# A two-layer decoder trunk: all products with the activations stationary, norms by rows, contracted operands turned on TensorE

## The chip, the cores and the metric

The kernel runs on one core of a Trainium2 chip, with its five engines: TensorE (matrix products and transposes), VectorE, ScalarE, GpSimd and SyncE, which issues most DMA transfers. The metric is device time in microseconds (us), the median of several runs.

## The reference

256 tokens of width 2048 pass two layers, in float32. Layer 0 is a gated spatial mixer, layer 1 attention with 16 heads of 128. With 256 tokens and key blocks of 256 every query's own block is the only one, so that layer is plain causal attention.

```
layer 0: u, v = gelu(x @ w_in[:, :4096]); z = x @ w_in[:, 4096:]
         v = layer_norm(v); s = tril(w_s[g]) @ v + b_s[g]     # 16 groups, 128-token chunks
         y = u * s * silu(z)
layer 1: q, k, v, z = x @ w_in;  y = causal_attention(q, k, v) * silu(z)
both:    x = layer_norm(alpha * x + y @ w_out[i])
         x = x + sigmoid(x @ w_gate[i]) * (p[i] @ w_proj[i])
```

## The kernel before

Weights stream through the core once, in 180 chunks of 128 x 2048 numbers (1 MiB). A chunk is loaded in two pieces by SyncE's queue into one of four buffers `wr` (L102), and every number is split exactly into hi (12 significant bits, `wh`, by ScalarE, L103) and lo (the rest, `wl`, by VectorE, L104). Loads and splits are issued two chunks ahead of the products (`AHEAD`); `wh` and `wl` have three buffers each. For the first two chunks of each gate matrix (`POOL_LO`) GpSimd makes the lo. A float32 product runs as three passes in a faster format, hi x hi, hi x lo and lo x hi, which add up in a bank of PSUM (eight banks of 128 x 512).

Activations lie feature-major, features on partitions and tokens along the row, except `v` in both layers. There are two kinds of products:

- `column_units` (L144 to L166, all its products have line L162): a chunk of 128 output columns and all 2048 input rows. The weights are stationary, the activations move. For each of the 16 contraction tiles one product with `wh` moves hi and lo of the activations together (512 columns), one with `wl` moves the hi alone (256): 32 products a chunk. The two halves of the bank are added on the way out by ScalarE and VectorE (`halves_sum`, L169, L170). u and z of layer 0, q, k and z of layer 1, w_out and the gate (`w_gate`) of both layers are made so, 144 chunks.
- `row_unit` (L172 to L198, products L184, L186, L188): the activations are stationary and the weights move, 512 columns at a time: 24 products a chunk. The output has tokens on partitions. Only `v` of layers 0 and 1 (banks `v`, `y`) is made so, 32 chunks.

The order of the program is that of the code, refined by a scheduler when the kernel is built. `tick` runs after every chunk of products, and `at(n, f)` puts `f` behind the n-th chunk from there: so the spatial mixing (`spatial`, L293, L294, after `mixing_bias`, L240, L241), the softmax steps of a head (`scores` L532 to L551, `probs` L557, `values` L572) run between products of other chunks. Each engine takes its instructions strictly in order.

The LayerNorm of a layer (`after`, from L336) is feature-major, so its sums run over partitions. VectorE and ScalarE gather sums of the residual and its square while w_out runs; a product with a matrix of 1/2048 (`st`, L412 to L414) gives the moments; `diag` (L424, L429), GpSimd's power (L427) and a product with ones (`rb`, L452) bring 1/sigma to all partitions. Meanwhile TensorE runs `embed`, p @ w_proj (L444 to L446, bank `pp`): five of its eight steps ahead of `rb`, three behind. Then `norm_pair` (L460 to L467) makes the input `xn` of the gate.

Of the kernel before, what the change touches and what calls it, by code (L numbers as in the profile page):

```python
# [30 lines left out]
NT4 = 21           # 4 KB tiles of activations on chip: (hi, lo) of what products take  # L31
NT2 = 18           # 2 KB tiles
# [7 lines left out]
def decoder_trunk(ctx: ExitStack, tc: tile.TileContext, xT, pT, wv_a, wu_a, wz_a, w_sT, b_s,  # L40
                  wv_b, wqkz_b, w_out, w_gate, w_proj, cols, out):
    """Activations lie feature-major ([features, tokens]) all the way, except v, by rows in both
    mixers. Every float32 product runs as three float32r passes: an operand is split exactly into
    hi (12 significant bits) + lo (the rest), and hi*hi + hi*lo + lo*hi add up in PSUM."""
# [4 lines left out]
    small = ctx.enter_context(tc.tile_pool(name="small", bufs=4))  # L49
    psum = ctx.enter_context(tc.tile_pool(name="psum", bufs=8, space=bass.MemoryType.PSUM))  # L50
# [6 lines left out]

    def bank(name):
# [20 lines left out]
    on_pool = set()  # L79
# [64 lines left out]
    def column_units(n, xs, step=KT, joined=False):  # L144
# [502 lines left out]
```

## Time and profile before

| | us |
|---|---|
| Median of three runs | 1076.09 (1075.79 to 1077.84) |
| Profiled execution, first to last instruction (span) | 1075.3 |
| TensorE busy | 1057.4 (98% of the span) |
| VectorE busy | 719.0 (67%) |
| ScalarE busy | 528.5 (49%) |
| GpSimd busy | 29.2 (3%) |
| DMA | 198.71 MB, mean 185 GB/s |

The profiled execution is one run of the program; its own time is known as the span, which lies 0.8 us under the median of the runs. Busy times are shares of the whole, over stages with different limits. A product's duration includes its way through the array, in which the next one already runs: prices of products are read from start to start, or from the chain.

### The profile page before, as it was taken

To read this page: it belongs to the slowest core of one execution; us is meant where nothing else is said; L and a number is where in the kernel's file an instruction comes from. 1 tells how busy PE (TensorE), PEld (TensorE's weight loads), DVE (VectorE), ACT (ScalarE), POOL (GpSimd) and SP (SyncE) were. 2 spreads that over 40 slices of the span, in tenths; PEclk is the share of its full clock that TensorE was granted. 3 is DMA by queue.
4 is the path that set the end of the run, shared out by engine and by line. 5 is a ranking of instruction groups with operands and counts; after the bars stand their busy time and mean duration, and the time that the engine had idled before them with its cause. 6 is when DMAs were issued, how large, how long until landed. Compare 5 with 4: busy or idle time off the path is not lost.

```text
span 1075.3 us, 15279 instructions
## 1 busy us (share of the span) xinstructions
PE 1057.4 (98%) x5946; PEld 918.8 (85%) x5946; DVE 719.0 (67%) x1103; ACT 528.5 (49%) x787; POOL 29.2 (3%) x28
## 2 busy tenths in 40 slices
PE   8999999999999989999999999999999999998998
PEld 6888888888888878888888888888888888897887
DVE  5567866756577988665545666666666566889664
ACT  5455534445534466554434654555555543456542
POOL 1100000000000040000000000000000000022000
PEclk9999999999999989999999999999999999998999
DMA  7984545455755526555555545444455555452761
GB/s 259 292 272 159 194 163 187 163 193 181 260 196 189 186 96 206 186 196 195 195 195 178 176 159 173 159 172 161 160 179 177 190 194 190 176 187 83 254 211 49
DMA packets 59000, 198.71 MB, mean 185 GB/s; under 512 B 6560, under 2 KB 8864, under 8 KB 58928
## 3 DMA queue, kind: packets, MB, share of 16 engines
q1 hardware_dynamic: 58896, 197.68, 53.2%
q8 instruction: 47, 0.77, 0.3%
q14 instruction: 25, 0.20, 0.1%
q0 software_dynamic: 32, 0.05, 0.0%
HBM read 195.61 MB, written 2.10 MB: 184 GB/s over the span
## 4 chain that ended last, share of the span: by engine, by line
PE 95%; DMA 2%; POOL 1%; DVE 1%; issue 1%; SPq 0%; ACT 0%; POOLq 0%; DVEq 0%
PE f L162 76%; PE y L188 3%; PE y L186 3%; PE y L184 3%; PE v L188 2%; PE v L186 2%; PE v L184 2%; POOL wl L104 1%; DVE diag L429 1%; PE ov L572 1%; DMA wr<-in_wv_a 1%; PE pt L557 0%; PE sp L293 0%; DMA xr<-in_xT 0%; DMA wsr<-in_w_sT 0%
## 5 line engine op out<-in xcount | busy, mean ns | idle before, releaser
L104 DVE TENSOR_TENSOR wl<-wr,wh 128x1024 fp32r<-128x1024 f32 (+1 forms) x358 | 424.7, 1203 | 153.5 <-ACT wh L103 152.0
L103 ACT ACTIVATE wh<-wr 128x1024 fp32r<-128x1024 f32 (+1 forms) x366 | 372.8, 1039 | 246.6 <-issue 119.8
L162 PE MATMUL f<-x,wh 128*128 128x512 f32 x1280 | 453.2, 398 | 0.0
L162 PE MATMUL f<-x,wl 128*128 128x256 f32 x1280 | 345.8, 280 | 0.0
L162 PEld LDWEIGHTS f<-x,wh 128*128 128x128 f32 x1280 | 238.2, 188 | 51.3
L162 PEld LDWEIGHTS f<-x,wl 128*128 128x128 f32 x1280 | 241.6, 189 | 5.6
L162 PE MATMUL f<-b,wh 128*128 128x512 f32 (+1 forms) x544 | 179.1, 385 | 0.0
L162 PE MATMUL f<-xn,wh 128*128 128x512 f32 (+1 forms) x544 | 178.8, 385 | 0.0
L162 PE MATMUL f<-b,wl 128*128 128x256 f32 x512 | 139.0, 281 | 0.0
L162 PE MATMUL f<-xn,wl 128*128 128x256 f32 x512 | 139.0, 281 | 0.0
L162 PEld LDWEIGHTS f<-b,wh 128*128 128x128 f32 x544 | 98.4, 188 | 19.6
L162 PEld LDWEIGHTS f<-xn,wh 128*128 128x128 f32 x544 | 98.2, 188 | 19.4
L169 ACT ACTIVATE fp<-f 128x256 f32<-128x256 f32 x78 | 29.3, 379 | 155.4 <-PE f L162 155.4
L162 PEld LDWEIGHTS f<-b,wl 128*128 128x128 f32 x512 | 96.7, 189 | 2.9
L162 PEld LDWEIGHTS f<-xn,wl 128*128 128x128 f32 x512 | 96.8, 189 | 2.8
L170 DVE TENSOR_TENSOR fp<-fp,f 128x256 f32<-128x256 f32 x78 | 32.4, 417 | 85.7 <-ACT fp L169 85.7
L104 POOL TENSOR_TENSOR wl<-wr,wh 128x1024 fp32r<-128x1024 f32 x8 | 19.7, 2478 | 845.8 <-ACT wh L103 845.8
L184 PE MATMUL y<-wh,x 128*128 128x512 f32 x128 | 40.7, 389 | 0.0
L188 PE MATMUL y<-wl,x 128*128 128x512 f32 x128 | 40.7, 389 | 0.0
L186 PE MATMUL y<-wh,x 128*128 128x512 f32 x128 | 40.7, 389 | 0.0
L184 PE MATMUL v<-wh,x 128*128 128x512 f32 x128 | 38.1, 393 | 2.6 <-ACT wh L103 2.6
L188 PE MATMUL v<-wl,x 128*128 128x512 f32 x128 | 37.3, 390 | 0.0
(149 smaller groups left out, 892.2 us busy)
## 6 DMA issues: line engine op xcount, KB each, us to landing
wr<-in_wqkz_b SPq DMA_DIRECT2D x96, 512.0 KB, 3.7
wr<-in_w_out SPq DMA_DIRECT2D x64, 512.0 KB, 3.8
wr<-in_w_gate SPq DMA_DIRECT2D x64, 512.0 KB, 4.2
wr<-in_wu_a SPq DMA_DIRECT2D x32, 512.0 KB, 3.8
wr<-in_wz_a SPq DMA_DIRECT2D x32, 512.0 KB, 3.8
wr<-in_wv_b SPq DMA_DIRECT2D x32, 512.0 KB, 3.8
wr<-in_wv_a SPq DMA_DIRECT2D x26, 512.0 KB, 5.6
wr<-in_w_proj SPq DMA_DIRECT2D x8, 512.0 KB, 3.8
```

Of the source, the lines that this page charges most:

```text
L103: nc.scalar.activation(hi[:, c], raw, AF.Copy)
L104: (nc.gpsimd if len(ready) in on_pool else nc.vector).tensor_sub(lo[:, c], raw, f32(hi[:, c]))
L162: nc.tensor.matmul(*m, start=k == 0 and j == 0, stop=k == KT - 1 and j == len(ms) - 1, skip_group_check=True)
L169: nc.scalar.activation(o, ps[:, 0:S], AF.Copy)
L170: nc.vector.tensor_add(o, o, ps[:, S:2 * S])
L184: nc.tensor.matmul(banks[m][n], xh, wh[:, i, n, :], start=first, stop=False)
L186: nc.tensor.matmul(banks[m][n], xl, wh[:, i, n, :], start=False, stop=False)
L188: nc.tensor.matmul(banks[m][n], xh, wl[:, i, n, :], start=False, stop=last)
L429: nc.vector.tensor_scalar(diag[:, m * P:(m + 1) * P], ident, rv[:, m:m + 1], None, op0=ALU.mult)
L572: nc.tensor.matmul(ov[:, n], vk[m][h // 4][:, a, hc], b, start=j == 0, stop=j == 4, skip_group_check=True)
```

## The change

All products become row-major, with the activations stationary and 512 columns of weights moving; `column_units` is gone. The weights lie in DRAM as before; for a matrix that is stored by columns, a chunk now holds 512 output columns (four blocks `b` of 128) of four contraction tiles `k` (`by_blocks`), so a load's rows are 2 KB where they were 4 KB, and a product's moving operand is four runs of 128 numbers that lie 512 numbers apart. `row_slice` takes four such chunks for 512 columns of all tokens. The results have tokens on partitions, so both norms take statistics along the row (`bn_stats`) and apply gain and bias from broadcast rows `gb`, which `gain_bias` loads by GpSimd's queue from a copy in DRAM (`vecs`). What is contracted next has to be feature-major again: `turn` transposes it on TensorE, four 128x128 tiles a bank, and splits it on the way out. x is turned into rows (`rows_of_x`), q and k of every head into columns (`head`), the output back into columns (`store`). The values product of attention is turned round too. `probs` follows `scores` by one chunk where it was two. GpSimd makes no weight's lo any more.

```diff
+    def by_blocks(w):
+        return [("p (b k c) -> p k b c", dict(b=4, k=4),
+                 w[4 * n:4 * n + 4, :, 512 * c:512 * c + 512].rearrange("b p e -> p b e"))
+                for n in range(NS) for c in range(4)]
+    def flat(src):
+        return [("", {}, src.rearrange("p (b e) -> p b e", b=4))]
...
-            nc.sync.dma_start(raw, src[:, c])
+            nc.sync.dma_start(raw.rearrange("p (b e) -> p b e", b=4 // parts), src[:, b])
             nc.scalar.activation(hi[:, c], raw, AF.Copy)
-            (nc.gpsimd if len(ready) in on_pool else nc.vector).tensor_sub(lo[:, c], raw, f32(hi[:, c]))
-        ready.append((hi, lo))
...
-    def column_units(n, xs, step=KT, joined=False):
...
-                for k in range(k0, k0 + step):
-                    lh = (ps[u][:, 0:S], wl[:, k, :], xs[k][:, 0, :])
...
-                    else:
-                        ms = [(ps[u], wh[:, k, :], xs[k].rearrange("p h s -> p (h s)"))]
-                        ms.insert(k < KT - 1, lh)
-                    for j, m in enumerate(ms):
-                        nc.tensor.matmul(*m, start=k == 0 and j == 0,
-                                         stop=k == KT - 1 and j == len(ms) - 1, skip_group_check=True)
...
-    def halves_sum(o, ps):
-        nc.scalar.activation(o, ps[:, 0:S], AF.Copy)
-        nc.vector.tensor_add(o, o, ps[:, S:2 * S])
...
+        nc.gpsimd.dma_start(vecs, t[0:6 * KT, 0:P])
+    def gain_bias(i, n):
+        t = r4("gb")
+        for j in range(2):
+            v = vecs[(2 * i + j) * KT + 4 * n:(2 * i + j) * KT + 4 * n + 4, :].rearrange("k c -> (k c)")
+            nc.gpsimd.dma_start(t[:, j, :], v.partition_broadcast(P))
+        return t
...
+        pat, kw, wh, wl = weights()
+        if pat:
+            wh, wl = ([w.rearrange(pat, **kw)[:, i] for i in range(len(ks))] for w in (wh, wl))
...
+            def o(n):
+                return banks[m][n].rearrange("p (b c) -> p b c", b=4) if pat else banks[m][n]
...
-                nc.tensor.matmul(banks[m][n], xh, wh[:, i, n, :], start=first, stop=False)
+                nc.tensor.matmul(o(n), xh, wh[i][n], start=first, stop=False)
...
+    def row_slice(xs, name="y"):
+        banks = [[bank(name)] for _ in range(NM)]
+        for c in range(4):
+            row_unit(banks, range(4 * c, 4 * c + 4), xs, both if c == 3 else None)
+        return [b[0] for b in banks]
...
+    def turn(xs, j, rows, n="t"):
+        tp = bank("tp")
+        for u in range(2):
+            f = 2 * j + u
+            for m in range(NM):
+                nc.tensor.transpose(tp[:, u * S + m * P:u * S + (m + 1) * P],
+                                    rows[f // 4][:, m, (f % 4) * P:(f % 4 + 1) * P], ident)
+        t = split(tp, n)
+        xs[2 * j:2 * j + 2] = [t[:, u] for u in range(2)]
...
+    def normalise(r, gb, m, mean, rstd):
+        o = r[:, m, :]
+        nc.vector.scalar_tensor_tensor(o, o, mean, gb[:, 0, :], op0=ALU.subtract, op1=ALU.mult)
+        nc.vector.scalar_tensor_tensor(o, o, rstd, gb[:, 1, :], op0=ALU.mult, op1=ALU.add)
...
-            for m in range(NM):
-                vh, vl = (vs[m][g // 4][:, j, (g % 4) * P:(g % 4 + 1) * P] for j in range(2))
-                nc.tensor.matmul(sp[:, m], vh, w, start=True, stop=False, skip_group_check=True)
-                nc.tensor.matmul(sp[:, m, 0, :], vl, w[:, 0, :], start=False, stop=True,
...
+            vh, vl = (vs[j][:, h, :, i * P:(i + 1) * P] for h in range(2))
+            for a, (wt, vt) in enumerate(((w[:, 0, :], vh), (w[:, 0, :], vl), (w[:, 1, :], vh))):
+                nc.tensor.matmul(sp[:, i], wt, vt, start=a == 0, stop=a == 2, skip_group_check=True)
...
+            nc.vector.scalar_tensor_tensor(o, sp[:, i], bsT[:, g:g + 1], o, op0=ALU.add, op1=ALU.mult)
...
+    vgb = [None] * NS
+    at(1, turn_vectors)
+    for n in range(NS):
+        at(1, lambda n: vgb.__setitem__(n, gain_bias(0, n)), n)
+        at(2 * n + 3, norm_v, n)
+    for j in range(KT // 2):
+        at(2 * j + 7, spatial, j)
...
+    def rows_of_x(n):
+        R[n] = r4("r")
+        raw = [t2("xq") for _ in range(2)]
+        for i in range(2):
+            nc.sync.dma_start(in2(raw[i]), xT[:, 4 * n + 2 * i:4 * n + 2 * i + 2, :])
...
+            tp = bank("tx")
...
+                nc.tensor.transpose(tp[:, f * P:(f + 1) * P],
+                                    raw[f // 2][:, (f % 2) * S + m * P:(f % 2) * S + (m + 1) * P], ident)
+            nc.scalar.activation(R[n][:, m, :], tp, AF.Copy)
...
-        at(2 * n + 1, norm_v, n)
-        at(2 * n + 2, mixing_bias, n)
...
-        at(2 * f + 5, spatial, f)
...
-        nc.tensor.matmul(st, f32(avg), acc, start=True, stop=False, skip_group_check=True)
-        nc.tensor.matmul(st[:, 0:S], f32(avg), rows(KT - 1), start=False, stop=False, skip_group_check=True)
-        nc.tensor.matmul(st[:, S:2 * S], f32(avg), q, start=False, stop=True, skip_group_check=True)
...
+        for n in range(NS):
+            at(2 + 3 * n, lambda n: gb.__setitem__(n, gain_bias(1 + i, n)), n)
+        for n in range(NS):
+            y = row_slice(br)
+            for m in range(NM):
+                r = R[n][:, m, :]
+                nc.vector.scalar_tensor_tensor(r, r, ALPHA, y[m], op0=ALU.mult, op1=ALU.add)
+                nc.vector.bn_stats(st[:, m, n, :], r)
...
-            nc.vector.scalar_tensor_tensor(diag[:, c], var[:, c], 1.0, ident, op0=ALU.mult, op1=ALU.mult,
-                                           accum_out=rv[:, m:m + 1])
...
-        nc.gpsimd.tensor_tensor(rv, rv, half, op=ALU.pow)
-        for m in range(NM):
-            nc.vector.tensor_scalar(diag[:, m * P:(m + 1) * P], ident, rv[:, m:m + 1], None, op0=ALU.mult)
...
+            nc.vector.bn_aggr(mv[:, m, :], st[:, m])
+        nc.vector.tensor_scalar(rs, mv[:, :, 1], EPS, None, op0=ALU.add)
+        nc.gpsimd.tensor_tensor(rs, rs, half, op=ALU.pow)
...
+            for k in range(2):
+                xh, xl = pk[:, k, 0, c], pk[:, k, 1, c]
+                nc.tensor.matmul(ps, xh, wp[0][:, k, n % 2, :], start=k == 0, stop=False)
+                nc.tensor.matmul(ps, xl, wp[0][:, k, n % 2, :], start=False, stop=False)
+                nc.tensor.matmul(ps, xh, wp[1][:, k, n % 2, :], start=False, stop=k == 1)
...
+        def norm_slice(n):
+            for m in range(NM):
+                normalise(R[n], gb[n], m, mv[:, m, 0:1], rs[:, m:m + 1])
+        units = [(n, m) for n in range(NS) for m in range(NM)]
+        for u in units[:5]:
+            embed(*u)
+        for n in range(2):
+            norm_slice(n)
+            turn(xn, 2 * n, R, "xn")
+            turn(xn, 2 * n + 1, R, "xn")
+            if n == 0:
+                for u in units[5:]:
+                    embed(*u)
+        def rest(n):
+            norm_slice(n)
+            turn(xn, 2 * n, R, "xn")
+            turn(xn, 2 * n + 1, R, "xn")
+        at(1, rest, 2)
+        at(2, rest, 3)
...
+            y = row_slice(xn, "g")
...
+                    c = slice(h * w, (h + 1) * w)
+                    r = R[n][:, m, c]
+                    nc.scalar.activation(t[:, c], y[m][:, c], AF.Sigmoid)
+                    nc.vector.tensor_mul(t[:, c], t[:, c], pp[n][:, m, c])
+                    nc.vector.tensor_add(r, r, t[:, c])
+            for h in range(2):
+                if not last:
+                    at(1 + h, turn, xo, 2 * n + h, R, "x2")
+                elif n < NS - 1:
+                    at(1 + h, store, 2 * n + h)
+                else:
+                    store(2 * n + h)
...
+                nc.tensor.transpose(tp[:, u * S + m * P:u * S + (m + 1) * P],
+                                    R[f // 4][:, m, (f % 4) * P:(f % 4 + 1) * P], ident)
+        t = t2("o")
+        nc.scalar.activation(t, tp, AF.Copy)
+        for u in range(2):
+            f = 2 * j + u
+            nc.sync.dma_start(out[f * P:(f + 1) * P, :], t[:, u * S:(u + 1) * S])
...
+    def head(h, q, k):
+        c = slice((h % 4) * HD, (h % 4 + 1) * HD)
+        tp = bank("tq")
+        for j, r in enumerate((q, k)):
+            for m in range(NM):
+                nc.tensor.transpose(tp[:, j * S + m * P:j * S + (m + 1) * P], r[:, m, c], ident)
+        at(1, scores, h, split(tp, "qk"))
...
-        at(2, probs, h, s)
+        at(1, probs, h, s)
...
-        steps = ((0, c0, 0, p[:, 0, c0]), (0, c0, 0, p[:, 1, c0]), (0, c0, 1, p[:, 0, c0]),
-                 (1, slice(P, 3 * P), 0, p[:, :, c1]), (1, slice(P, S), 1, p[:, 0, c1]))
...
-    br = gated(oT)
-    after(1, br, x0)
+        for m, bs in ((0, (0,)), (1, (1, 2))):
+            steps = [(b, x, y) for b in bs for x, y in ((0, 0), (0, 1), (1, 0))]
+            for a, (b, x, y) in enumerate(steps):
+                nc.tensor.matmul(ov[:, m], p[:, x, b * P:(b + 1) * P], vk[b // 2][h // 4][:, y, hc],
...
+        nc.scalar.activation(o[h // 4][:, :, hc], ov[:, 0:NM], AF.Copy)
...
+    for n in range(NS):
+        rows = []
+        for _ in range(2):
+            y = row_slice(xs, "qk")
+            rows.append(r4("qk"))
+            for m in range(NM):
+                nc.scalar.activation(rows[-1][:, m, :], y[m], AF.Copy)
+        for h in range(4):
+            at(1 + 2 * h, head, 4 * n + h, *rows)
```

The order on the engines that wait or are waited for moves at three places. TensorE, before, at the LayerNorm (w_out's last products, `st` the moments, `pp` embedding, `rb` the broadcast of 1/sigma):

```order
L162 MATMUL f<-b,wl 128x256
L412 MATMUL st<-acc,avg 128x512
L413 MATMUL st<-x_2504,avg 128x256
L444 MATMUL pp<-p,wh 128x256
L414 MATMUL st<-q,avg 128x256
L445 MATMUL pp<-p,wh 128x256
L446 MATMUL pp<-p,wl 128x256
...
L452 MATMUL rb<-diag,ones 128x256
L444 MATMUL pp<-p,wh 128x256
```

The dots stand for the rest of five steps of embedding. TensorE now, at the same place, behind the first 27 embedding products (L235 are the transposes of the norm's output; the dots stand for four more embedding products):

```order
L419 MATMUL pp<-wl,p 128x512
L235 MATMUL tp<-ident,r 128x128 x2
L417 MATMUL pp<-wh,p 128x512
L418 MATMUL pp<-wh,p 128x512
...
L235 MATMUL tp<-ident,r 128x128 x6
L417 MATMUL pp<-wh,p 128x512
```

The products of the moments and of `rb` are gone; transposes stand between the embedding steps, and wait for VectorE's output `r` itself.

VectorE, before, from the last column of w_out to the diagonal (`x` the residual, `mv` the moments):

```order
L397 TENSOR_TENSOR x_2504<-x_2504,f 128x256
L460 TENSOR_TENSOR x_2497<-x_2497,mv 128x512
L419 SCALAR_TENSOR_TENSOR mv<-st,mv 128x256
L460 TENSOR_TENSOR x_2498<-x_2498,mv 128x512
L424 SCALAR_TENSOR_TENSOR diag,rv<-mv,ident 128x128 x2
L460 TENSOR_TENSOR x_2499<-x_2499,mv 128x512
L426 TENSOR_SCALAR rv<-rv 128x2
L460 TENSOR_TENSOR x_2500<-x_2500,mv 128x512
L429 TENSOR_SCALAR diag<-ident,rv 128x128 x2
L460 TENSOR_TENSOR x_2501<-x_2501,mv 128x512
```

VectorE now, from the last bank of w_out (`r` the residual by rows, `y` the bank, `rs` 1/sigma, `wl` the splits of gate weights):

```order
L397 SCALAR_TENSOR_TENSOR r<-r,y 128x512
L122 TENSOR_TENSOR wl<-wr,wh 128x1024
L398 BN_STATS st<-r 128x6
L122 TENSOR_TENSOR wl<-wr,wh 128x1024
L400 BN_AGGR mv<-st 128x2
L303 SCALAR_TENSOR_TENSOR r<-r,mv,gb 128x512
L401 TENSOR_SCALAR rs<-mv 128x2
L303 SCALAR_TENSOR_TENSOR r<-r,mv,gb 128x512
L304 SCALAR_TENSOR_TENSOR r<-r,rs,gb 128x512
L122 TENSOR_TENSOR wl<-wr,wh 128x1024
L304 SCALAR_TENSOR_TENSOR r<-r,rs,gb 128x512
L122 TENSOR_TENSOR wl<-wr,wh 128x1024
```

Weight splits of the gate now stand between the operations of the norm, where GpSimd had them.

TensorE in attention, before, at the end of a chunk (`pt` probabilities of one head, `sc` scores of the next):

```order
L557 MATMUL pt<-ident,sm 128x128 x3
L532 MATMUL sc<-qk 128x2x128
L533 MATMUL sc<-qk 128x128
L535 MATMUL sc<-qk 128x256
L536 MATMUL sc<-qk 128x256
L537 MATMUL sc<-qk 128x256
L162 MATMUL f<-x_3662,wh 128x512
L162 MATMUL f<-x_3662,wl 128x256
```

TensorE in attention now, behind two chunks that follow each other (the dots stand for the 24 products of the second; `tq` is q and k of a head, `ov` the values product):

```order
L507 MATMUL tq<-ident,qk 128x128 x4
L542 MATMUL pt<-ident,sm 128x128 x3
...
L517 MATMUL sc<-qk 128x2x128
L518 MATMUL sc<-qk 128x128
L520 MATMUL sc<-qk 128x256
L521 MATMUL sc<-qk 128x256
L522 MATMUL sc<-qk 128x256
L555 MATMUL ov<-vk,pb 128x128 x9
```

The scores of a head and its transposed probabilities are one chunk apart, and transposes of the next head stand ahead of the latter.

## Rows read from the trace of the kernel before

**Rows 1.** The profile's page: TensorE's busy time, and the chain by line.
```profile
PE 1057.4 (98%) x5946; PEld 918.8 (85%) x5946; DVE 719.0 (67%) x1103; ACT 528.5 (49%) x787; POOL 29.2 (3%) x28
...
PE f L162 76%; PE y L188 3%; PE y L186 3%; PE y L184 3%; PE v L188 2%; PE v L186 2%; PE v L184 2%; POOL wl L104 1%; DVE diag L429 1%; PE ov L572 1%; DMA wr<-in_wv_a 1%; PE pt L557 0%; PE sp L293 0%; DMA xr<-in_xT 0%; DMA wsr<-in_w_sT 0%
```

**Rows 2.** The chain in order of time: start us, length us, what.
```profile
212.16 124.28 PE f L162 x704
```

**Rows 3.** TensorE's timeline, last chunk of `v` and the next: start us, length us.
```profile
90.53 0.39 PE L184 MATMUL v<-wh,x 128*128 128x512 f32 x1
...
95.97 0.39 PE L162 MATMUL f<-x,wh 128*128 128x512 f32 x1
```

**Rows 4.** TensorE's timeline, layer 0's LayerNorm.
```profile
376.19 1.02 PE L412 MATMUL st<-acc,avg 128*128 128x512 f32 x2
...
390.30 1.19 PE L452 MATMUL rb<-diag,ones 128*128 128x256 f32 x2 [4.80 <-DVE diag L429]
...
397.08 0.40 PE L162 MATMUL f<-xn,wh 128*128 128x512 f32 x1
```

**Rows 5.** VectorE's timeline, end of the program.
```profile
1072.05 0.48 DVE L488 SCALAR_TENSOR_TENSOR x<-x,col,sg 128x256 f32<-128x256 f32 x1
```

**Rows 6.** Durations, ns min/median/max, by source line: the mixing products, then `y`.
```profile
L240 PE MATMUL rs<-ws,ones x4: 394/394/394, 107.3 to 144.1; 128*128 128x512 f32 x4
...
L241 PE MATMUL rs<-ws,ones x4: 390/390/390, 107.5 to 144.4; 128*128 128x512 f32 x4
...
L186 PE MATMUL y<-wh,x x128: 389/389/389, 487.9 to 574.0; 128*128 128x512 f32 x128
```

**Rows 7.** The chain in attention, from 640.9 us.
```profile
641.40 0.33 PE pt L557 x3
...
647.97 0.54 PE ov L572 x5
```

**Rows 8.** TensorE's timeline in attention, the same transposes.
```profile
641.24 0.49 PE L557 MATMUL pt<-ident,sm 128*128 128x128 f32 x3
641.49 0.36 PE L532 MATMUL sc<-qk 128*128 128x256 f32 x1
```

**Rows 9.** Durations of the transposes (same view as rows 6).
```profile
L557 PE MATMUL pt<-ident,sm x48: 270/272/273, 603.2 to 794.5; 128*128 128x128 f32 x48
```

**Rows 10.** The chain in the u stage, from 118 us.
```profile
119.11 0.23 PE rs L240
...
125.13 0.12 PE sp L293
...
126.01 0.63 PE f L162 x3
```

**Rows 11.** Stretches: length, busy us (instructions) PE PEld DVE ACT POOL, PEclk, DMA share, GB/s.
```profile
3.00:10.00 7.00, 6.25 (x27) 4.92 (x27) 4.56 (x8) 4.62 (x9) 0.38 (x2) 1.00 0.92 306
490.00:574.00 84.00, 84.00 (x372) 69.55 (x371) 42.49 (x43) 34.94 (x39) 0.00 (x0) 1.00 0.55 194
390.30:394.50 4.20, 4.20 (x18) 4.02 (x19) 4.20 (x10) 1.32 (x3) 0.00 (x0) 0.50 0.43 157
```

**Rows 12.** Timelines of GpSimd and VectorE, layer 0's LayerNorm.
```profile
377.46 5.20 POOL L104 TENSOR_TENSOR wl<-wr,wh 128x1024 fp32r<-128x1024 f32 x2 [275.28 <-ACT wh L103]
...
385.50 4.66 DVE L429 TENSOR_SCALAR diag<-ident,rv 128x128 f32<-128x128 f32 x2 [0.59 <-POOL rv L427]
390.07 2.48 DVE L460 TENSOR_TENSOR x<-x,mv 128x512 f32<-128x512 f32 x4
```

**Rows 13.** Groups of the page: busy us, mean ns of one | idle before, releaser.
```profile
L104 DVE TENSOR_TENSOR wl<-wr,wh 128x1024 fp32r<-128x1024 f32 (+1 forms) x358 | 424.7, 1203 | 153.5 <-ACT wh L103 152.0
```

**Rows 14.** DMA issues: count, KB each, median us to landing.
```profile
bs<-in_b_s SPq DMA_DIRECT2D x4, 256.0 KB, 7.2
```

**Rows 15.** VectorE's timeline in attention, one softmax.
```profile
657.01 0.55 DVE L539 TENSOR_TENSOR sm<-sc,causal 128x384 f32<-128x384 f32 x1
...
661.07 0.55 DVE L551 TENSOR_SCALAR sm<-sm,sum 128x128 f32<-128x128 f32 x2
```

More of the change, by code (lines that the diff above doesn't have):

```diff
@@ L30 @@
 WARM = 7
-NT4 = 21
-NT2 = 18
+NT4 = 20
+NR4 = 12
+NT2 = 5
 def f32(ap):
@@ L198, in row_unit @@
         tick()
+    both = [(m, 0) for m in range(NM)]
+    def row_slice(xs, name="y"):
[12 more added lines that the diff above has]
+        xs[2 * j:2 * j + 2] = [t[:, u] for u in range(2)]
     warm = bank("warm")
@@ L210, in load_x @@
             nc.sync.dma_start(in2(raw), xT[:, k:k + 2, :])
-            xs[k:k + 2] = of_two(split(raw, "x"))
+            t = split(raw, "x")
+            xs[k:k + 2] = [t[:, u] for u in range(2)]
             return
@@ L232, in load_mixing @@
         ws[j] = split(raw, "ws", 4)
-        bs[j] = t2("bs")
-        nc.sync.dma_start(bs[j], b_s[c].partition_broadcast(P))
-    def mixing_bias(j):
-        rp = bank("rs")
-        rp4 = rp.rearrange("p (g t) -> p g t", g=4)
-        nc.tensor.matmul(rp4, ones, ws[j][:, :, 0, :], start=True, stop=False)
-        nc.tensor.matmul(rp4, ones, ws[j][:, :, 1, :], start=False, stop=True)
-        q4[j] = t2("q4")
-        for i in range(4):
-            c = slice(i * P, (i + 1) * P)
-            nc.vector.scalar_tensor_tensor(q4[j][:, c], rp[:, c], col[:, 1, 4 * j + i:4 * j + i + 1],
-                                           bs[j][:, c], op0=ALU.mult, op1=ALU.add)
     load_x(0)
@@ L276, in norm_v @@
+    vs = [None] * (KT // 2)
     def norm_v(n):
         for m in range(NM):
[L278 to L302 removed]
@@ L320, in gelu_u @@
[L320 to L341 removed]
+            normalise(v[n], vgb[n], m, vmv[:, m, 0:1], vrs[:, m:m + 1])
@@ L344, in after @@
+    for n in range(NS):
+        at(4 * n + 4, rows_of_x, n)
+    br = gated(us, xs)
+    def after(i, br):
         ps_ = t2("pr")
         nc.sync.dma_start(in2(ps_), pT[i])
-        pk = of_two(split(ps_, "p"))
-        acc = t2("acc")
-        sd, sq = acc[:, 0:S], acc[:, S:2 * S]
-        def rows(f):
-            return R[f // 2][:, (f % 2) * S:(f % 2 + 1) * S]
-        acc0 = t2("acc0")
-        c0 = acc0[:, 0:S]
-        shift = acc0[:, S:2 * S]
-        H = KT // 2
-        def square(f, q):
-            nc.scalar.activation(q, rows(f), AF.Square)
@@ L427, in after @@
-        nc.gpsimd.tensor_tensor(rv, rv, half, op=ALU.pow)
-        for m in range(NM):
-            nc.vector.tensor_scalar(diag[:, m * P:(m + 1) * P], ident, rv[:, m:m + 1], None, op0=ALU.mult)
+        pk = split(ps_, "p")
+        st = small.tile([P, NM, NS, 6], F32, name="st")
+        mv = small.tile([P, NM, 2], F32, name="mv")
+        rs = small.tile([P, NM], F32, name="rs")
+        gb = [None] * NS
+        for n in range(NS):
+            at(2 + 3 * n, lambda n: gb.__setitem__(n, gain_bias(1 + i, n)), n)
@@ L471, in after @@
-        for j in range(KT // 2):
-            norm_pair(j)
-            if len(pp) < KT // 2:
-                embed(len(pp))
-        xo = []
-        def emit(j, t):
-            nc.scalar.activation(t, t, AF.Sigmoid)
-            nc.vector.tensor_mul(t, t, pp[j])
-            for u in range(2):
-                finish(2 * j + u, t[:, u * S:(u + 1) * S])
-            if i < DEPTH - 1:
-                xo.extend(of_two(split(R[j], "x2")))
-        def finish(f, t):
-            r = rows(f)
-            nc.vector.scalar_tensor_tensor(r, r, bcol[:, f:f + 1], t, op0=ALU.add, op1=ALU.add)
-            if i == DEPTH - 1:
-                nc.sync.dma_start(out[f * P:(f + 1) * P, :], r)
@@ L507, in decoder_trunk, with embed @@
-    xs = after(0, br, x0)
+        def embed(n, m):
+            if m == 0:
+                pp.append(r4("pp"))
+                if n % 2 == 0:
+                    wp[:] = [t.rearrange("p (k n c) -> p k n c", k=2, n=2) for t in weights(1 + n // 2)[2:]]
+            ps = bank("pp")
+            c = slice(m * P, (m + 1) * P)
+            for k in range(2):
[3 more added lines that the diff above has]
+                nc.tensor.matmul(ps, xh, wp[1][:, k, n % 2, :], start=False, stop=k == 1)
+            nc.scalar.activation(pp[n][:, m, :], ps, AF.Copy)
@@ L511, in decoder_trunk @@
+    xs = after(0, br)
     vk = [[None] * NS for _ in range(NM)]
```

311 lines of the change are left out of this document (108 added, 203 removed).

## The prediction

> **What bounds the kernel now.** I read the page first: TensorE is busy for 98% of the span, and the chain that ended last is TensorE nearly throughout, three quarters of it on the one line of the column products [rows 1]. So a change pays by shortening TensorE's own work, or the few places where TensorE stands still; what ScalarE and VectorE save is worth nothing unless TensorE waits for them there. Then I read the chain in order of time, for the price of a chunk of weights. A column chunk is 32 products: 704 of them in one unbroken piece took 124.28 us [rows 2], 5.649 us a chunk. A row chunk is 24 products of 512 columns: from the first product of the last chunk of `v` to the product that follows the chunk is 5.44 us [rows 3]. Both stream 12,288 columns; the row chunk does it in fewer instructions. Last I read the stretch around a LayerNorm, the one place in the middle of the program where TensorE stands [rows 4], and the tail, where VectorE ends the program [rows 5].
>
> **The change, part by part.** The sum is made against the profiled execution's span of 1075.3 us; the median of the three runs, 1076.09, lies 0.8 above, which I add at the end.
>
> *Products.* 144 chunks (u 16, z 16, q and k 32, z 16, w_out 32, gate 32) change from column to row chunks: 144 x (5.649 - 5.44) = -30.1 us. The new row chunk isn't quite the one that I timed: its moving operand is four runs of 128 columns, 2 KB apart. The nearest rows are the old mixing products, whose moving operand skips too: 394 ns for the first of a pair and 390 for the second, against 389 for the plain row product [rows 6]. The second follows one of its own kind and so is the nearer; I take no extra. At the bound of 394, 5 ns more on 144 x 24 products give back 17.3 us.
>
> *Transposes.* 290 are added: six activations of 32 each (the gated branch and the norm's output in both layers, layer 0's output, the stored output), 32 that turn x into rows, 64 for q and k of 16 heads, 2 for the vectors. The kernel has three in a row for every head already. The chain gives these three 0.33 us, 0.11 each [rows 7]; from the first start to the start of the instruction behind them it is 0.25, 0.083 each [rows 8]. The short group pays for its entry, and a group of four or eight less so: I take 0.10 each, 29.0 us, with 24.1 and 31.9 as the bounds. Their evictions lie on ScalarE and VectorE beside the chunk of products that runs between a transpose and the product that takes it.
>
> The duration of one such transpose is 272 ns [rows 9], but three start within 0.25 us, so most of that duration overlaps the next. The Trainium skill ("TensorE: Matmul & The Clock Gate", Part 4: PE-mode transpose) gives about 275 ns for a 128x128 transpose in a kernel's context; the duration agrees. By the page's figure as a price, 290 transposes would be an estimated 80 us, and the change a clear loss.
>
> *Values.* Five products become nine of 128 columns for each head. Nine at 0.083 to 0.11 are 0.75 to 0.99 us, against 0.54 for the five [rows 7]. I take 0.82, +4.5 us over 16 heads.
>
> *Mixer A.* Now the eight spatial products of a pair of groups take 0.88 us, from 125.13 to 126.01; afterwards it is six of 256 columns, at the row's 0.12 each 0.72: -1.3 us over eight pairs. The eight mixing products of 0.23 go: -1.8 [rows 10].
>
> *LayerNorm.* From the last product of w_out to the first of the gate TensorE now takes 20.9 us [rows 4]: statistics products, 96 embedding products, 4.8 us of standing still, and then 4.2 us at a granted clock of 0.50, the lower of the two levels [rows 11]. The standing still is VectorE's: two 128x128 operations take 4.66 us while GpSimd splits a weight piece, and GpSimd's two pieces before that hold 5.20 us [rows 12]. All of this goes. What is late next is the new chain on VectorE. Behind the last product and ahead of the first transpose stand four operations of 512 columns (0.62 each, by four in 2.48 us [rows 12]), two weight splits of 1.2 [rows 13] and four small ones with GpSimd's power between them, for which I allow 1.6: 6.5 us. TensorE has five embedding units ahead of that transpose, 30 products of 0.227 or 6.8 us, so VectorE is just in time. The second half of the slice is behind one more split and costs some 0.3; slices 1 and 2, with splits between their operations, cost as much or a little more. I take 1.5 us of waits a layer, with 0 and 5 (today's wait) as the bounds. The stage is then 48 products of 512 columns, 10.9 us, and 1.5: 12.4 against 20.9, or -17.0 us over two layers; its transposes are counted above. The power on GpSimd is queued behind the gain and bias loads, of which the last pair is issued five chunks earlier, some 27 us; were it late, the whole norm would wait behind it.
>
> *VectorE's queue elsewhere.* In the u stage the first normalisation waits for gain and bias: a turned copy goes out to DRAM and comes back broadcast, both on GpSimd's queue. A broadcast load of that size took 7.2 us to land [rows 14]. With the first chunk (5.4), the turning (1.5) and a write that I put at half a load (3.6), it is there about 18 us into the stage. Behind it in VectorE's queue stand the splits of chunk 4, which TensorE takes at 22: hidden, but the backlog that follows is tight. I allow 1 us, with 6 as the bound. In attention `probs` now comes one chunk after `scores`, not two. The softmax between them takes 4.6 us on VectorE and ScalarE with one split in it, from the first row of it to the end of the last [rows 15]; a second split makes it 5.8. TensorE covers that with the values products (0.8), a chunk (5.44) and the next head's four transposes (0.4). One head in four has its order the other way round and loses part of the cover. I allow 1.5 us in all, with 16 (1 us a head) as the bound.
>
> *DMA.* Column weights arrive in rows of 2 KB instead of 4 KB. From 3 to 10 us, when all rows are of 2 KB or less, the queues moved 306 GB/s at a share of 0.92, or 333 at full share; with 4 KB rows it is 194 at 0.55, or 353 [rows 11]. The need is 193 (1 MiB in 5.44 us), so nothing is late, and the edit costs nothing. The four weight splits a layer that leave GpSimd are among VectorE's above.
>
> *Tail.* Now a sigmoid, two VectorE operations (0.48 for one of 256 columns [rows 5]) and a store follow the last product. Afterwards it is twice that in two halves, of which one more of each adds some 0.35 on ScalarE and 0.7 on VectorE, then transposes (0.4), a copy (0.6) and stores: +2.3 us with the second store's issue.
>
> The sum: -30.1 + 29.0 + 4.5 - 3.1 - 17.0 + 1.0 + 1.5 + 2.3 = -11.9. Span 1063.4, time 1064.2 us.
>
> **The rivals.** (a) The skipping operand costs 394 ns and not 389. Place: the 3,456 products of the changed chunks; price 17.3 us; time 1081.5, slower. It decides from 3.4 ns a product (11.9 us over 3,456). For it speaks the first mixing product of each pair, against it the second. Chance 0.15. (b) Each transpose holds TensorE for its whole 272 ns: 290 x 0.17 more, 49 us, 1113. The rows' starts speak against it; the page named above for it. 0.03. (c) The order of VectorE's queue becomes the wait: a late gain load (6), 1 us a head (16), 5 us a norm. Half of what these bounds lie above my allowances (5 + 14.5 + 7) is 13, which makes 1077, no difference; the first or the last alone leaves a gain. 0.20. (d) The gain is larger: transposes at 0.083 and none of the waits, -4.9 and -5.5: 1053.8. 0.10. (e) 2 KB rows move at half the rate, so that 193 GB/s need a share of 1.1, and TensorE loses a tenth of 144 chunks, 78 us: 1142. The start speaks against it. 0.02.
>
> **How the numbers follow.** The forecast's own range, 1058 to 1070, has 0.50. A range that leaves no more than 2 in 10 out goes from (d)'s 1054 to 1079, part of the way into (a). 0.2% is about what a measurement of this kernel can tell from no change, so faster means below 1073.9 and slower above 1078.2. Faster takes the forecast, (d), half of (c) and a fifth of (a), 0.73; same takes the other half of (c), 0.10; slower the rest, 0.17.
>
> **What would show it.** Right: chunks of 5.44 us at every row product in the chain; about 0.4 us for four transposes; 13 to 15 us from the last w_out product to the first gate product, without `diag` rows, without a wait of over 1 us and without a granted clock of 0.50. Wrong: products of 394 ns and chunks of 5.56; `pt` transposes that wait for VectorE in attention; a wait for `gb` in the u stage; a lower clock among the transposes.

## The result and the profile after

The changed kernel takes 1070.30 us (1069.59 to 1071.11), the one before 1076.61 beside it: ratio 0.9934, 95% interval 0.9919 to 0.9949, so it is 0.7% faster. The forecast was 1064.2 with a range of 1054 to 1079. The sign is right, the gain about half of the forecast: the profiled span went from 1075.3 to 1068.9 us, by 6.4, where the sum gave 11.9.

The page of the changed kernel, TensorE's busy time, and the chain by line:

```profile
PE 1057.5 (99%) x4944; PEld 878.1 (82%) x4944; DVE 616.8 (58%) x763; ACT 499.5 (47%) x659; POOL 24.5 (2%) x46
...
PE 82%; issue 14%; DMA 2%; DVE 1%; ACT 0%; POOL 0%; SPq 0%; POOLq 0%; ACTq 0%; DVEq 0%
PE qk L204 5%; PE g L208 5%; PE qk L208 5%; PE qk L206 5%; PE g L206 5%; PE g L204 5%; PE y L206 5%; PE y L204 5%; PE y L208 5%; PE z L204 4%; PE z L206 4%; PE z L208 4%; PE u L206 3%; PE u L204 3%; PE u L208 3%
```

TensorE is still the bound [rows 1], and busy for as long as before: what the fewer product instructions and the norms saved, the transposes and the longer values products took. By the page the gain is the time in which it stood still, 17.9 us of the span before and 11.4 now; time at a lower clock counts as busy. Where the microseconds come from has to be read stage by stage. The stages below run from the start of the first instruction of one to that of the next on TensorE's timeline (in the changed kernel at 95.96, 370.75, 383.62, 476.27, 564.28, 956.13, 968.98 and, the end of the last product, 1061.80 us). Other runs of the same code repeat all but the first to 0.1 us. The forecast column is the sum's terms, laid out by stage; ten of the norm's transposes a layer stand in its own stage, the others in the gate's.

| stage | before | after | change | forecast |
|---|---|---|---|---|
| start and v of layer 0 | 95.97 | 95.96 | 0.0 | 0 |
| u, z, w_out of layer 0 | 280.22 | 274.79 | -5.4 | -5.5 |
| LayerNorm 0, embedding | 20.89 | 12.87 | -8.0 | -7.5 |
| gate 0 | 90.34 | 92.65 | +2.3 | +1.3 |
| v of layer 1 | 87.05 | 88.01 | +1.0 | +0.8 |
| q, k, z, attention, w_out of layer 1 | 384.86 | 391.85 | +7.0 | +2.2 |
| LayerNorm 1, embedding | 21.11 | 12.85 | -8.3 | -7.5 |
| gate 1 | 90.70 | 92.82 | +2.1 | +1.3 |
| tail | 4.17 | 7.09 | +2.9 | +3.1 |

Behind the start the change costs time in every stage but the two norms and layer 0's mixer (u, z, w_out). In the mixer the chain shows one of the eight spatial groups, six products in 0.71 us where eight took 0.88 [rows 10]:

```profile
134.48 0.71 PE sp L329 x6
```

VectorE's first normalisation in that stage waits for gain and bias (`gb`) until 112.86, 16.9 us into it:

```profile
112.86 0.75 DVE L303 SCALAR_TENSOR_TENSOR v<-v,vmv,gb 128x512 f32<-128x512 f32 x1 [7.95 <-DMA gb<-vecs]
```

TensorE does not wait for it. The waits of TensorE in the changed kernel, without those of the start (engine, line, releaser: us in total, times, longest):

```profile
PE to L476 <- DVE r L460: 1.4, 1, 1.4
PE tp L235 <- DVE r L304: 1.2, 2, 0.6
PE pt L542 <- DVE sm L536: 0.5, 1, 0.5
```

None is large: of the 9.6 us that `rb` waited for `diag` in two layers, 1.2 are left, in front of the norm's transposes. The norm stages as windows (length, busy us of PE, PEld, DVE, ACT, POOL, granted clock, DMA share, GB/s):

```profile
370.75:383.62 12.87, 12.29 (x59) 9.72 (x58) 12.26 (x19) 8.99 (x14) 1.15 (x1) 1.00 0.52 171
956.13:968.98 12.85, 12.28 (x59) 9.72 (x58) 12.24 (x19) 8.99 (x14) 1.14 (x1) 1.00 0.54 172
```

The granted clock is 1.00 all through, where it was 0.50 behind `rb` [rows 11].

The price of a group of four transposes, on TensorE's timeline: an undisturbed chunk in the u stage, from its first product to the next chunk's, then the gate.

```profile
107.12 0.39 PE L204 MATMUL u<-wh,x 128*128 128x512 f32 x1
...
112.56 0.39 PE L204 MATMUL u<-wh,x 128*128 128x512 f32 x1
```

```profile
413.28 0.39 PE L208 MATMUL g<-wl,xn 128*128 128x512 f32 x1
413.51 0.60 PE L235 MATMUL tp<-ident,r 128*128 128x128 f32 x4
413.87 0.48 PE L204 MATMUL g<-wh,xn 128*128 128x512 f32 x1
414.18 0.40 PE L206 MATMUL g<-wh,xn 128*128 128x512 f32 x1
...
419.44 0.60 PE L235 MATMUL tp<-ident,r 128*128 128x128 f32 x4
```

The group starts at 413.51, the product behind it at 413.87: 0.36 us. But that product needs 0.31 to the next start instead of 0.227, and a few behind it start 0.23 apart; the chunk of 24 products takes 5.57 us (413.87 to 419.44) where 24 undisturbed ones take 5.44. A group of four costs 0.35 + 0.13 = 0.48 us, 0.12 a transpose. Not everything that stands between two chunks does this as much: behind the six spatial products a chunk takes 5.47.

### The profile page after: what moved, and what is told of

The parts are those of the page before. It is cut to its first block, busy times and chain, and to the rows that moved or that the text cites. A ratio compares the mean times of both kernels' runs of the same rounds, so it can differ in the third digit from the quotient of the medians.

```text
span 1068.9 us, 12836 instructions
## 1 busy us (share of the span) xinstructions
PE 1057.5 (99%) x4944; PEld 878.1 (82%) x4944; DVE 616.8 (58%) x763; ACT 499.5 (47%) x659; POOL 24.5 (2%) x46
## 4 chain that ended last, share of the span: by engine, by line
PE 82%; issue 14%; DMA 2%; DVE 1%; ACT 0%; POOL 0%; SPq 0%; POOLq 0%; ACTq 0%; DVEq 0%
PE qk L204 5%; PE g L208 5%; PE qk L208 5%; PE qk L206 5%; PE g L206 5%; PE g L204 5%; PE y L206 5%; PE y L204 5%; PE y L208 5%; PE z L204 4%; PE z L206 4%; PE z L208 4%; PE u L206 3%; PE u L204 3%; PE u L208 3%
## 5 line engine op out<-in xcount | busy, mean ns | idle before, releaser
L204 PE MATMUL g<-wh,xn 128*128 128x512 f32 x256 | 101.7, 397 | 0.0
L204 PE MATMUL z<-wh,x 128*128 128x512 f32 x256 | 101.4, 396 | 0.0
L204 PE MATMUL qk<-wh,x 128*128 128x512 f32 x256 | 101.3, 396 | 0.0
L204 PE MATMUL y<-wh,b 128*128 128x512 f32 x256 | 100.1, 391 | 0.0
L208 PE MATMUL g<-wl,xn 128*128 128x512 f32 x256 | 100.0, 391 | 0.0
L208 PE MATMUL qk<-wl,x 128*128 128x512 f32 x256 | 100.0, 391 | 0.0
L208 PE MATMUL z<-wl,x 128*128 128x512 f32 x256 | 100.0, 390 | 0.0
L206 PE MATMUL qk<-wh,x 128*128 128x512 f32 x256 | 99.9, 390 | 0.0
L206 PE MATMUL z<-wh,x 128*128 128x512 f32 x256 | 99.8, 390 | 0.0
L206 PE MATMUL g<-wh,xn 128*128 128x512 f32 x256 | 99.8, 390 | 0.0
L208 PE MATMUL y<-wl,b 128*128 128x512 f32 x256 | 99.7, 389 | 0.0
L206 PE MATMUL y<-wh,b 128*128 128x512 f32 x256 | 99.6, 389 | 0.0
L204 PEld LDWEIGHTS y<-wh,b 128*128 128x128 f32 x256 | 48.1, 188 | 9.9
L206 PEld LDWEIGHTS y<-wh,b 128*128 128x128 f32 x256 | 48.1, 188 | 9.7
L206 PEld LDWEIGHTS g<-wh,xn 128*128 128x128 f32 x256 | 48.2, 188 | 9.5
```

The source lines that it names most:

```text
L204: nc.tensor.matmul(o(n), xh, wh[i][n], start=first, stop=False)
L206: nc.tensor.matmul(o(n), xl, wh[i][n], start=False, stop=False)
L208: nc.tensor.matmul(o(n), xh, wl[i][n], start=False, stop=last)
```

## The experiments

**GpSimd's lo: each half of the change alone.** To the kernel before:

```diff
-POOL_LO = (0, 1)
+POOL_LO = ()
```

> The kernel before with one part of the change alone: VectorE makes the lo of the first two gate chunks too, GpSimd none. Theory (the two engines slow each other): the two diag operations that took 4.66 us beside GpSimd's split fall well under 1 us each, the standing still ahead of rb falls from 4.8 us to 0 to 2.5, and with it most of the 4.2 us at clock 0.50 that cost half their length. That is 4 to 7 us a layer, 1062 to 1069 us. Rival (the queue): the four splits of 1.2 us now stand between the norm's operations in VectorE's queue and put off diag by as much as it gained; 1075 to 1078 us, and the whole gain of the changed kernel's norm would then come from the norm by rows.

Measured: 1065.40 us, ratio 0.9895 (0.9878 to 0.9913). This one line alone gains 10.6 us, more than the whole change. VectorE's timeline in layer 0's norm:

```profile
380.13 0.68 DVE L460 TENSOR_TENSOR x<-x,mv 128x512 f32<-128x512 f32 x1
...
383.11 0.48 DVE L429 TENSOR_SCALAR diag<-ident,rv 128x128 f32<-128x128 f32 x2 [0.59 <-POOL rv L427]
383.50 2.49 DVE L460 TENSOR_TENSOR x<-x,mv 128x512 f32<-128x512 f32 x4
```

The two `diag` operations take 0.48 us, not 4.66 [rows 12]; `rb` no longer waits, and the stage falls from 20.89 to 13.90 us. The clock doesn't fall either. As windows (columns as above), the stage, and the stretch whose clock was 0.50 [rows 11]; then TensorE's waits:

```profile
376.18:390.08 13.90, 13.90 (x107) 13.01 (x105) 12.48 (x25) 9.76 (x17) 1.07 (x1) 1.00 0.45 152
390.30:394.50 4.20, 4.08 (x23) 3.32 (x22) 4.20 (x12) 4.20 (x9) 0.00 (x0) 1.00 0.28 109
```

```profile
PE f L162 <- DVE wl L104: 1.1, 2, 0.5
```

So of the 7.0 us, 4.8 are the wait, and an estimated 2.1 what TensorE lost in the 4.2 us behind it at the lower of its two clock levels, half of full speed. The rival is seen only behind the stage: the first gate chunks wait 0.55 us a layer for VectorE's lo, and gate 0 takes 91.61 us for 90.34; the rest of that difference isn't assigned. The other way round, in the changed kernel:

```diff
+    on_pool = set()
...
+        on_pool.update(len(chunks) + f for f in POOL_LO)
         chunks += by_blocks(w_gate[i])
...
-            nc.vector.tensor_sub(lo[:, c], raw, f32(hi[:, c]))
+            (nc.gpsimd if len(ready) in on_pool else nc.vector).tensor_sub(lo[:, c], raw, f32(hi[:, c]))
```

> The changed kernel with the lo of the first two gate chunks back on GpSimd. Theory (they slow each other): VectorE's normalising operations of 512 columns, 0.75 us now, get up to twice as long while GpSimd splits, GpSimd's pieces take some 2.6 us each and come late for the first gate products; TensorE's wait ahead of the first transposes, 0.58 us now, becomes 2 to 5: 1073 to 1080 us. Rival (the queue): VectorE has 4.8 us less to do a layer, the 0.58 us goes, 1069 to 1070 us.

Measured: 1087.15 us, ratio 1.0097 (1.0080 to 1.0113). The row-major kernel that keeps GpSimd's share is slower than the kernel before, and slower than was expected: the operations were to take up to twice as long, and take over three times. VectorE and GpSimd in its first norm, then TensorE's waits, then the norm as windows:

```profile
370.42 1.41 DVE L305 SCALAR_TENSOR_TENSOR r<-r,mv,gb 128x512 f32<-128x512 f32 x2
371.75 0.68 DVE L399 SCALAR_TENSOR_TENSOR r<-r,y 128x512 f32<-128x512 f32 x1
372.35 2.49 DVE L305 SCALAR_TENSOR_TENSOR r<-r,mv,gb 128x512 f32<-128x512 f32 x1
374.77 0.68 DVE L400 BATCH_NORM_STATS2 st<-r 128x6 f32<-128x512 f32 x1
375.37 2.29 DVE L305 SCALAR_TENSOR_TENSOR r<-r,mv,gb 128x512 f32<-128x512 f32 x1
...
379.30 6.24 DVE L306 SCALAR_TENSOR_TENSOR r<-r,rs,gb 128x512 f32<-128x512 f32 x3 [0.61 <-POOL rs L404]
```

```profile
371.90 5.21 POOL L124 TENSOR_TENSOR wl<-wr,wh 128x1024 fp32r<-128x1024 f32 x2 [229.96 <-ACT wh L123]
...
379.24 5.08 POOL L124 TENSOR_TENSOR wl<-wr,wh 128x1024 fp32r<-128x1024 f32 x2
```

```profile
PE tp L237 <- DVE r L306: 13.5, 4, 4.5
```

```profile
370.00:382.00 12.00, 7.74 (x35) 6.07 (x33) 11.28 (x12) 6.67 (x9) 9.10 (x5) 0.99 0.41 147
382.00:392.00 10.00, 7.52 (x30) 6.17 (x31) 9.96 (x13) 2.81 (x5) 2.32 (x1) 0.67 0.32 105
```

A normalising operation, 0.7 us alone (two in 1.41), takes 2.49 and 2.29 us, and ends just after GpSimd's piece does (by 0.55 us each time); of the three that take 6.24, the first two take 2.82 each and the third, with no piece beside it, 0.74. `bn_stats` (L400) beside the same piece keeps its 0.68, and so does L399, which takes one of its inputs from PSUM. So GpSimd's split holds up the VectorE operations that read two tensors in SBUF, but not the `bn_stats`, nor the one with an input in PSUM. `diag` [rows 12] read only one large input and was held as well. TensorE waits 13.5 us for them in two layers, and behind the wait it runs at a lower clock here too (0.67 on average from 382 to 392 us); the two norm stages together are 17.8 us longer than in the changed kernel.

The Trainium skill ("SBUF — State Buffer", section "SBUF: two separate sides") says that GpSimd and VectorE arbitrate for one pair of ports, which a GpSimd instruction or a VectorE one in a two-port mode or with two inputs in SBUF holds for its whole length while the other is blocked. The rows agree, with 2.49 us for 0.70 beside GpSimd pieces of some 2.6; what mode `diag` runs in no trace here shows.

Together with the two main kernels the runs make a square: columns with GpSimd's lo 1076.0, without 1065.4; rows with it 1087.2, without 1070.3 us. All of the change but GpSimd's lo costs 4.9 us without GpSimd's share and 11.1 with it.

**The same work of GpSimd elsewhere.** In the changed kernel as above, with

```diff
+POOL_LO = (8, 9)
```

> The changed kernel with the lo of gate chunks 8 and 9 on GpSimd, where in a_lo_pool it was 0 and 1: the same four pieces of 2.6 us a layer, away from the norm. Theory (GpSimd's split holds up VectorE wherever it is, but that costs only where TensorE waits for VectorE's result): no more waits of TensorE than in the changed kernel, 1069.5 to 1071.5 us. Rival (the split by GpSimd is itself late, or costs wherever it is): as in a_lo_pool, up to 17 us more, 1087.

Measured: 1071.27 us, ratio 0.9947 (0.9930 to 0.9964). Every stage behind the start is as long as in the changed kernel, to 0.1 us (gate 0 92.63), though VectorE is held up here too. GpSimd's second pair of pieces, and VectorE:

```profile
428.43 4.75 POOL L124 TENSOR_TENSOR wl<-wr,wh 128x1024 fp32r<-128x1024 f32 x2 [1.16 <-ACT wh L123]
```

```profile
430.87 2.86 DVE L461 TENSOR_TENSOR sg<-sg,pp 128x512 f32<-128x512 f32 x1 [7.24 <-ACT sg L460]
433.77 0.69 DVE L462 TENSOR_TENSOR r<-r,sg 128x512 f32<-128x512 f32 x1
434.38 1.22 DVE L124 TENSOR_TENSOR wl<-wr,wh 128x1024 fp32r<-128x1024 f32 x1
435.51 0.68 DVE L461 TENSOR_TENSOR sg<-sg,pp 128x512 f32<-128x512 f32 x1
```

The profiled run's span is 1.9 us longer for a start that took 2.0 longer (95.5 to 98.0 us in all runs, while the first chunks land). GpSimd holds VectorE up in either place, and it costs where TensorE waits for VectorE's next result. The run is a mild test of that: VectorE had little to do beside these pieces, and one operation a layer (2.86 and 2.91 us) was held.

**The price of a transpose.** In `turn`:

```diff
-        for u in range(2):
+        for u in (0, 1, 0, 1):
```

> The changed kernel with every group of four transposes of turn made twice into the same bank: 160 transposes more, in groups of eight where they were of four. Theory (the sum's missing microseconds are the transposes' price): in the changed kernel's trace a group of four costs 0.48 us, 0.35 up to the next product and 0.13 by which the 24 products behind it take longer than 5.44, and a group of eight of rows_of_x 0.79 and 0.10 to 0.14; so 0.41 to 0.45 more for each of 40 groups, 16 to 18 us, 1086 to 1089 us. Rival 1 (0.083 each, as between the starts in the kernel before): 13.3 us, 1083.5. Rival 2 (272 ns each): 43 us, 1114.

Measured: 1087.33 us, ratio 1.0101 (1.0081 to 1.0121); the span is 1085.0, 16.1 more than the changed kernel's, and the stages behind the start are 16.6 longer: 0.104 us for each of 160. So one more transpose in a group costs 0.10, as in the sum, and a group of eight (the last row here) is 0.79 to the next product:

```profile
449.54 1.03 PE L235 MATMUL tp<-ident,r 128*128 128x128 f32 x8
450.33 0.48 PE L204 MATMUL g<-wh,xn 128*128 128x512 f32 x1
```

What the sum lacked is a group's own price: 0.48 = 4 x 0.10 + 0.08. To see that apart:

```diff
-                at(1 + i, turn, br, 2 * n + i, o, "b")
+                at(1, turn, br, 2 * n + i, o, "b")
...
-                    at(1 + h, turn, xo, 2 * n + h, R, "x2")
+                    at(1, turn, xo, 2 * n + h, R, "x2")
...
-                    at(1 + h, store, 2 * n + h)
+                    at(1, store, 2 * n + h)
```

> The changed kernel with the two groups of four transposes of a slice (gated branch, layer 0's output, stored output) behind the same chunk, as one group of eight: 15 groups fewer, no transpose fewer. Theory (0.10 us a transpose and 0.08 a group, from groups of two, four and eight): 15 x 0.08 = 1.2 us less over the stages that hold them, 0.3 of it before the first norm, 0.3 between the first norm and v of layer 1, 0.3 from the first q to the second norm, 0.2 behind it. Rival (0.12 us a transpose in groups of any size): no stage shorter by over 0.1.

Measured: one run of 1069.06 us, too little to tell by; by stages 0.29 us less from u to w_out, 0.25 in gate 0 and 0.08 in v, 0.21 from q to w_out, 0.25 in gate 1: 1.08 for 15 groups, 0.07 a group. As expected.

**The operand that skips, the short rows.** Laid out on the host so that a chunk is four tiles of 512 columns:

```diff
-        return [("p (b k c) -> p k b c", dict(b=4, k=4),
...
+        return [f for n in range(KT) for f in flat(w[n])]
...
-        return lay(w.reshape(w.shape[0] // P, P, w.shape[1] // P, P).transpose(2, 1, 0, 3)).reshape(
+        return lay(w.reshape(4, 4, P, w.shape[1] // 512, 512).transpose(3, 0, 2, 1, 4)).reshape(
             w.shape[1] // P, P, -1)
```

> The changed kernel with the weights of the 144 changed chunks laid out in DRAM so that a chunk is 4 tiles of 512 columns: the moving operand is one run of 512 numbers, a load's rows are 4 KB again. Theory (neither costs anything): products start 0.227 us apart in the changed kernel, as in v; 1069 to 1071 us. Rival (the skipping operand or the short rows cost): up to 17 us less, 1053.

Measured: 1070.30 us, as the changed kernel, and no stage differs by over 0.1 us. Gate products in the changed kernel, then in this one (ns, min/median/max):

```profile
L204 PE MATMUL g<-wh,xn x256: 387/389/487, 383.6 to 1061.0; 128*128 128x512 f32 x128
```

```profile
L202 PE MATMUL g<-wh,xn x256: 387/389/482, 383.7 to 1061.0; 128*128 128x512 f32 x128
```

Rivals (a) and (e) fall: four runs of 128 numbers stream as one of 512 does (median 389 ns in both), and rows of 2 KB arrive in time.

**The lag of the softmax.**

```diff
-        at(1, probs, h, s)
+        at(2, probs, h, s)
```

> The changed kernel with probs two chunks behind scores, as before. Theory (VectorE keeps up with one chunk of cover): the trace shows one wait of 0.5 us for the softmax in 16 heads; 1069.5 to 1070.5 us. Rival (waits in attention are what is missing): 3 to 5 us less, 1065 to 1067 us.

Measured: 1069.84 us, not to be told from 1070.30; the attention stage is 0.9 us shorter (390.99). So waits in attention are not what is missing.

**Attention's mixer as before.** Of the changed kernel (the functions `column_units`, `halves_sum`, `scores` and `values` are those of the kernel before, and `probs` is again two chunks behind `scores`):

```diff
-            chunks += by_blocks(wqkz_b[2 * KT:3 * KT])
+            for h in range(KT):
+                chunks += flat(wqkz_b[h]) + flat(wqkz_b[KT + h])
+            for f in range(KT):
+                chunks += flat(wqkz_b[2 * KT + f])
...
-            y = row_slice(xs, "qk")
+        t = t2("qk")
+        for j in range(2):
+            halves_sum(t[:, j * S:(j + 1) * S], column_units(1, xs)[0])
```

> The changed kernel with the attention mixer of before: q, k and z of layer 1 by column_units, the head's scores and values feature-major, no transposes of q, k and the gated branch there; all else by rows. Theory: between the first q product and layer 1's last w_out product the changed kernel takes 391.9 us and the one before 385.1, though w_out is 3 us shorter; so this part of the change lost some 10 us, and undoing it gives 1060 to 1062 us. By terms: 96 transposes at 0.12 are 11.5, the values 6.6, against 10.0 for 48 chunks, 8.1 us. Rival (the recorded prices, 0.10 and 0.28 us a head more for the values, no waits): 9.6 and 4.5 against 10.0, 4.1 us, 1066.

Measured: 1057.65 us, ratio 0.9823 (0.9807 to 0.9838): 12.7 less than the changed kernel, all of it in the stage from q to w_out (379.10 us for 391.85). More than expected. One head's values in the changed kernel's chain, then in this kernel's timeline:

```profile
645.54 0.95 PE ov L555 x9
```

```profile
649.54 0.69 PE L579 MATMUL ov<-pb,vk 128*128 128x256 f32 x5
650.07 0.45 PE L200 MATMUL f<-x,wh 128*128 128x512 f32 x1
...
655.67 0.49 PE L564 MATMUL pt<-ident,sm 128*128 128x128 f32 x3
```

Nine products of 128 columns take 0.95 us where five took 0.53 (649.54 to 650.07): 6.6 us over 16 heads. The 96 transposes come to 11.5 at 0.12. Against that stand 48 column chunks. In this kernel those of q and k take 5.60 (650.07 to 655.67, behind the values) or 5.56, so they cost less than the 5.649 of [rows 2]; in the kernel before two heads of three had 5.65 and 5.71. From the first q product to w_out this kernel needs 292.05 us and the one before 294.12 for the same instructions; why is open. In the changed kernel, in turn, the chunks behind a head's scores and values take 5.47 to 5.54 us, not 5.44 (one takes 6.14, with the softmax's wait in it), some 1.1 us over 16 heads. So, roughly, 6.6 + 11.5 + 1.1 less 7.8 (16 chunks at 5.56, 16 at 5.60, 16 at 5.649, each against 5.44) are 11.4 of the 12.7; 0.9 more is what the longer lag of the softmax gave, and 0.4 isn't assigned.

**x and the output by rows.** The host hands x in a second time, laid out by rows, and takes the output by rows; all turns of x and of the output go:

```diff
-        raw = [t2("xq") for _ in range(2)]
...
+        nc.sync.dma_start(R[n], xr[:, :, 512 * n:512 * n + 512])
...
                     nc.vector.tensor_add(r, r, t[:, c])
+                    if last:
+                        nc.sync.dma_start(out[m * P:(m + 1) * P, 512 * n + h * w:512 * n + h * w + w], r)
```

> The changed kernel with x also given by rows (loaded straight into the residual) and the output stored by rows: 64 transposes, their evictions and copies are gone. Theory (transposes cost 0.12 with what they do to the products behind them): four groups of eight at 0.9 and seven of four at 0.48 are 7.0 us; in the tail six of eight transposes (0.9) and two copies (1.1) are gone too: 9 us, 1061 to 1062 us. Rival (the transposes are nearly covered, the loss lies in waits of VectorE): 2 us, of the tail, 1068.

Measured: 1062.28 us, ratio 0.9858 (0.9841 to 0.9874), 8.0 less than the changed kernel: 3.6 from u to w_out, 3.0 in gate 1, 2.0 in the tail by the stages, 8.6 together. That is 0.3 us above the range expected. The tail that it shortens, on the changed kernel's chain:

```profile
1061.57 0.25 PE g L208
...
1061.84 0.39 ACT sg L458
...
1062.25 0.76 DVE sg L459 x2
1063.01 0.35 DVE r L460
...
1063.40 0.90 PE to L476 x6
```

**Both together.**

> Both: the attention mixer of before in the changed kernel, and x and the output by rows. The two parts touch different stages, so the gains add up if both theories hold: 8 to 10 and 9 us, 1051 to 1054 us. Rival: as above with the recorded prices and covered transposes, 4 and 2 us, 1064.

Measured: 1048.66 us, ratio 0.9731 (0.9716 to 0.9745), against the 1049.6 that the two gains give when they are added; less than the 1051 to 1054 expected, since attention's mixer had gained more than expected. The stages are those of the two kernels, unchanged. It is the fastest of all: 28.7 us under the kernel before beside it (1077.37), 21.6 under the changed one.

## Why the prediction was right, and where its size was off

- **Products: right.** Row chunks of the changed kernel take 5.44 us wherever nothing else stands among them or just before them; the skipping operand costs nothing.
- **Transposes: mis-sized.** The step was to price 290 at "0.10 each", with the entry of a short group as what "a group of four or eight less so" pays. 0.10 is the price of one more in a group; each group costs 0.08 besides, which shows in the products behind it and not between its own starts [rows 8]. At 0.12 the term is 34.8 us instead of 29.0 (a little less for the groups of eight): 5.8 us, the largest of the misses. The forecast's 0.10 came close to one part of the price, and lacked the other.
- **Values: mis-sized.** 0.41 us more a head (0.95 against 0.54), not 0.28: 6.6 us, not 4.5. The chunks behind the values are longer as well, 1.1 us that the sum did not have.
- **Waits: allowed for too much.** The first normalisation in the u stage cost TensorE nothing (1.0 allowed); gain and bias landed 16.9 us into the stage, where 18 had been worked out. Attention has one wait of 0.5 (1.5 allowed, 0.9 by the run with the longer lag).
- **LayerNorm: the size nearly right, its cause only by half.** -17.0 without transposes was forecast, and -16.3 measured with the 20 that stand in the two stages. The prediction named the mechanism, VectorE slowed while GpSimd splits, but put the whole of it to the change as one. 14.2 of the 16.3 come with the one line on GpSimd's lo; with the gate counted in, rows and their transposes gain nothing at layer 0 (norm and gate without GpSimd's lo: 105.51 us in columns, 105.52 in rows) and gain 0.2 at layer 1 (105.84 and 105.67).
- **Tail: nearly right**, 2.9 us with its eight transposes, where 3.1 was forecast.
- **The rivals.** (a) and (e) fell by the flat layout, (b) by the doubled transposes, (c) by the list of waits and the longer lag. The larger gain (d) needed 0.083 a transpose.

With these sizes the sum is -11.9 + 5.8 (transposes) + 2.1 (values) + 1.1 (chunks behind them) - 2.0 (waits) - 1.7 (norms, -18.7 without their transposes) - 0.3 (tail, 2.0 without its transposes) = -6.9; the spans give -6.4. The 0.5 between them isn't assigned. Misses of both signs cancel in part, so that the total came nearer than its largest terms: to that extent its nearness is luck (the inner range, 1058 to 1070, just missed the time). And the sign hangs on the one line: with GpSimd's lo kept, the same row-major kernel is slower than the one before.

## What to carry to other kernels

Split a change that has several parts along its mechanisms before it is priced: here one line gained 10.6 us and everything else lost 4.9, and the sum of both looked like a success of the whole. Price work that is put among products by the time from the last product before it to one well behind it, since the products that follow pay too. Keep an operand's layout where its consumer wants it: turning attention's operands on TensorE, with the longer values products, cost more than the row products saved there, turning x and the output cost 8.0 us, and the kernel without those turns was the fastest of those run.

## What the runs showed of the hardware

Two things went beyond what the prediction took from the trace. VectorE operations with two inputs in SBUF, and `diag`, last until just after GpSimd's concurrent piece (0.7 us became 2.3 to 2.9, for `diag` 0.24 became 2.3), while a `bn_stats` and an operation with one input in PSUM beside such a piece ran at their usual 0.68. And a group of fp32 transposes slows the products behind it: the first one starts its successor 0.31 us later instead of 0.227, and a chunk of 24 takes longer than its 5.44, by nearly as much behind eight transposes (5.54) as behind four (5.57).
